# Hybrid attention trunk with 64 experts: the rank of a token is mapped to a partition in steps of seven

## Chip, core and metric

One Trainium2 chip, one core. The metric is device time in microseconds (us), the median of the runs shown. Nothing else runs on the chip.

## What is computed

A batch of one sequence: 2048 tokens of width 1024, behind 16 learned meta tokens. One layer:

1. `u = rmsnorm(h)`, `z = u @ w_in`; `z` is split for two groups of heads. Four heads are gated linear attention over chunks of 64 (`gla_group`), four are latent attention with softmax (`mla_group`). Both outputs go through `w_out` and are added to `h`.
2. `rmsnorm(h)` is routed in two steps: the best of 8 groups, then the best 2 of the 8 experts of that group, with gates from the two softmaxes. Each of the 64 experts is a SwiGLU of width 512, and its output times the gate is added to `h`:

```
hdn = silu(xb @ w_gate[e]) * (xb @ w_up[e])
out[token] += gate * (hdn @ w_down[e])
```

3. A last `rmsnorm`, without the meta tokens.

All is float32. Every token has two experts, so there are 4096 pairs of token and expert. Routing the given inputs by the reference gives between 23 and 109 tokens for an expert, 64 on average. No expert has more than the 112 that a block of the kernel holds.

## The kernel before

The program runs in phases. `phase_z` makes `z`, `phase_g` the linear attention, `phase_mix` the latent attention, the output projection and the routing. `phase_moe` runs the 64 experts, in the order group 0's first expert, group 1's first, and so on. Float32 products are made of two halves each, `hi` (the value rounded to a shorter type) and `lo` (the rest), three matmuls for one.

**Routing.** For each pair of token and expert the kernel counts how many earlier tokens chose that expert: the rank. A row of numbers `iob` (128 partitions by `BS` = 112 columns, the same in every partition) is written once, on GpSimd, at line 761. At line 1035 each rank is compared with `iob`: `R` has a one in the column whose number is the rank. Matmuls with `R` on the left (lines 1046, 1110 and 1113) then carry token number, gate, norm factor and a flag (is this expert the token's first) to the partition that has the number of that column. The results are `rt["src"]` and `tab`: for each expert a column of 112 partitions. A partition with no token keeps the number 2048, which lies past the last row.

```
1035:  R[:, k] = (rank[:, k, js, None] == iob)      # in short
1680:  B = [block(xsb[i % XSB], ..., rt["src"][:, e:e + 1], e, i) ...]
```

**Rows of tokens.** Each expert has four indirect DMAs, issued by GpSimd, all with one token row (4 KB) to a partition and 112 partitions: `gather(S.xs, S.src, ud)` reads the normed rows, `gather(S.b, S.src, hz)` reads the sums so far, `spread(hz, zd, S.z)` writes the new sums for the tokens whose first expert this is, `spread(out, od, S.o)` writes the finished rows for the others. A row number past 2047 moves no row (`bounds_check`). So an expert with n tokens moves n rows in `xs`, n in `b`, and n in `hz` and `out` together. The rank decides which of the 112 partitions have a row.

**Weights.** An expert has six tiles `raw` of 1 MB (128 partitions by 8 KB): gate, up and down, two each. SyncE loads them (line 1320) into a ring of six (`RAWB`); a load is issued once its buffer has been read. ScalarE makes `hi` of a tile, VectorE makes `lo` (line 1335 and the `Ordered` wrapper, whose instructions all have line 124), TensorE multiplies. The second `down` tile is used as float32, without halves. Per expert that is 60 matmuls of 512 columns in halves (48 `pg`, 12 `pd`), 8 float32 passes (`pd<-raw,hc`), and 12 transposes (8 `pt`, 4 `pth`).

**Order.** `moe_plan` writes one list of the instructions of all engines for the 64 experts; each engine runs its own in that order. On VectorE the small instructions that TensorE needs (`xl`, the low half of the turned token rows, and `hl`) stand between the large `lo`.

The loop `For_i(0, again, 1)` behind the experts serves experts of more than 112 tokens; here it runs no pass. It uses `iob` too (line 1766).

Of the kernel before, what the change touches and what calls it, by code (L numbers as in the profile page):

```python
# [34 lines left out]
BS = 112  # L35
# [40 lines left out]
def build(tc, a, dbg=None, stop=99):  # L76
    nc = tc.nc
    dbg = dbg or {}
    with ExitStack() as top:
# [23 lines left out]
        with ExitStack() as ctx:  # L103
            env["ctx"] = ctx
            env["keep"] = ctx.enter_context(tc.tile_pool(name="keep", bufs=1))
            z_rest, z_close = phase_z(**env)
            env["right"] = right = ExitStack()
            kvp = right.enter_context(tc.tile_pool(name="kv", bufs=1, side=RIGHT))
            env["kv"] = ([kvp.tile([P, L], F32R, name=n) for n in ("ch", "cl", "kr_")]
                         + [kvp.tile([P, NT + 1, P], F32R, name=n) for n in ("vh", "vl")])  # L110
            g_rest, g_close = phase_g(z_rest=z_rest, z_close=z_close, **env)
            phase_mix(g_rest=g_rest, g_close=g_close, **env)
            phase_moe(**env)
# [644 lines left out]
def phase_mix(tc, nc, a, qd, qrd, hg, ud, hz, xlist, xexp, kv, ident, ones, eps, rt, keep, ctx, right, g_rest, g_close, **_):  # L758
    ch, cl, kr_, vh, vl = kv
    iob = keep.tile([P, 1, BS], F32, name="iob")  # L760
    nc.gpsimd.iota(iob, pattern=[[0, 1], [1, BS]], base=0, channel_multiplier=0, allow_small_or_imprecise_dtypes=True)
    ids = keep.tile([P, 2, NT], F32, name="ids")
    nc.gpsimd.iota(ids, pattern=[[SEQ, 2], [P, NT]], base=-FAR, channel_multiplier=1, allow_small_or_imprecise_dtypes=True)
    rank = keep.tile([P, 2, NT], F32, name="rank")
# [1115 lines left out]
```

## Time and profile before

| | us |
|---|---|
| median of 3 runs (lowest, highest) | 2520.22 (2518.09, 2521.58) |
| profiled execution | 2517.44 |
| its span, first to last instruction | 2515.7 |
| mean granted TensorE clock | 0.98 |

The profile comes from one execution. A row of a group gives its busy time and what ended the idle time before it. Matmuls overlap, so the duration of one is longer than the distance from one to the next; how fast TensorE really goes is read from the starts in the timeline. The experts take the second half of the span: `silu` of the first starts at 1222.8 us, that of the 64th at 2479.9 us.

### The profile page before, as it was taken

The numbers are of one execution on the slowest core, as the hardware profiler recorded it, in microseconds if no ns is written. First come the engines' busy times: TensorE is split into PE (matmuls) and PEld (weight loads), VectorE is DVE, ScalarE is ACT, GpSimd is POOL, SyncE is SP. The second block draws the span as 40 slices with busy tenths as digits, with TensorE's granted clock in tenths as the row PEclk, the third lists the DMA queues.
The fourth block names the chain that finished last, engine by engine and source line by source line (L and its number), as shares of the span: only waits on it lengthen the run. The fifth ranks groups of instructions, "written<-read, shape, count | busy, mean of one in ns | idle before, by whom it ended". The sixth has DMA issues, their size and how long they took to land. (4 is left out here: it accounts for less than half of the span.)

```text
span 2515.7 us, 35600 instructions
## 1 busy us (share of the span) xinstructions
PE 2371.7 (94%) x12897; PEld 1876.6 (75%) x12897; DVE 1761.5 (70%) x2756; ACT 1307.3 (52%) x2018; POOL 816.6 (32%) x740
## 2 busy tenths in 40 slices
PE   7999998899999999998799999999999999999997
PEld 7899997687789999898566666666666666676664
DVE  6334244777577777776677778887877788787785
ACT  5112103554365555555466666666665666666663
POOL 0000003621001111112355545454445544454443
PEclk9999999899999999999799999999999999999999
DMA  6212116554412122113899999999999999999994
GB/s 208 74 59 80 54 44 174 174 173 143 165 55 77 60 68 71 65 51 141 251 368 361 349 352 353 358 353 361 355 342 350 344 351 360 354 348 363 344 358 182
DMA packets 161154, 571.70 MB, mean 227 GB/s; under 512 B 37132, under 2 KB 79644, under 8 KB 111820
## 3 DMA queue, kind: packets, MB, share of 16 engines
q1 hardware_dynamic: 125612, 509.71, 56.9%
q0 software_dynamic: 32912, 50.94, 6.3%
q10 hardware_dynamic: 2448, 8.72, 1.1%
q8 instruction: 103, 1.69, 0.3%
q14 instruction: 79, 0.65, 0.1%
HBM read 529.71 MB, written 106.63 MB: 253 GB/s over the span
## 5 line engine op out<-in xcount | busy, mean ns | idle before, releaser
L124 ACT CAST hi<-raw 128x2048 fp32r<-128x2048 f32 x318 | 607.0, 1909 | 444.0 <-DMA raw<-in_w_gate_dram 216.8
L124 DVE TENSOR_TENSOR lo<-raw,hi 128x2048 fp32r<-128x2048 f32 x317 | 723.5, 2287 | 136.4 <-ACT hi L124 131.1
L124 PE MATMUL pg<-hi,xl 128*112 128x512 f32 x1024 | 415.6, 406 | 50.1 <-DVE xl L124 50.1
L124 PE MATMUL pg<-hi,xh 128*112 128x512 f32 x1024 | 435.5, 425 | 2.0 <-ACT xh L124 1.8
L124 PE MATMUL pg<-lo,xh 128*112 128x512 f32 x1024 | 406.6, 397 | 0.0
L124 POOL DMA_INDIRECT hz<-z,t_zd x64 | 195.1, 3049 | 463.1 <-DVE z L124 454.4
L124 PEld LDWEIGHTS pg<-hi,xl 128*112 128x112 f32 x1024 | 181.6, 177 | 125.0 <-DVE xl L124 67.2
L124 PEld LDWEIGHTS pg<-hi,xh 128*112 128x112 f32 x1024 | 182.1, 178 | 73.5 <-ACT xh L124 15.1
L124 PEld LDWEIGHTS pg<-lo,xh 128*112 128x112 f32 x1024 | 182.8, 179 | 68.0 <-issue 7.8
L124 PE MATMUL pd<-raw,hc 128*112 128x512 f32 x512 | 230.0, 592 | 0.0
L135 PE MATMUL ps<-uh,wh 128*128 128x256 f32 (+3 forms) x768 | 219.1, 286 | 0.7 <-ACT uh L223 0.7
L136 PE MATMUL ps<-ul,wh 128*128 128x256 f32 (+3 forms) x768 | 218.8, 285 | 0.0
L137 PE MATMUL ps<-uh,wl 128*128 128x256 f32 (+3 forms) x768 | 218.0, 284 | 0.0
L124 PEld LDWEIGHTS pd<-raw,hc 128*112 128x112 f32 x512 | 90.0, 176 | 104.2 <-issue 97.0
L124 DVE SCALAR_TENSOR_TENSOR o<-z,ss,gain 112x1024 f32<-112x1024 f32 x64 | 82.2, 1285 | 118.5 <-POOL ss L124 118.5
L124 POOL DMA_INDIRECT out_dram<-o,t_od x64 | 121.3, 1895 | 105.0 <-DVE hl L124 88.8
L124 POOL DMA_INDIRECT xs<-ud,src x64 | 136.3, 2130 | 44.6 <-PE pt L124 22.3
L135 PEld LDWEIGHTS ps<-uh,wh 128*128 128x128 f32 (+1 forms) x768 | 145.2, 189 | 1.5 <-ACT uh L223 1.1
L136 PEld LDWEIGHTS ps<-ul,wh 128*128 128x128 f32 (+1 forms) x768 | 145.2, 189 | 0.6 <-DVE ul L224 0.2
L137 PEld LDWEIGHTS ps<-uh,wl 128*128 128x128 f32 (+1 forms) x768 | 145.3, 189 | 0.1
L257 DVE COPY st<-ps 128x256 f32<-128x256 f32 (+1 forms) x64 | 27.0, 422 | 145.7 <-PE ps L137 145.7
L338 POOL TENSOR_SCALAR_AFFINE_SELECT mf<-ones 128x128 f32<-128x128 f32 x2 | 0.6, 302 | 380.2 <-PE ps L137 380.2
(2413 smaller groups left out, 5340.8 us busy)
## 6 DMA issues: line engine op xcount, KB each, us to landing
raw<-in_w_gate_dram SPq DMA_DIRECT2D x128, 1024.0 KB
raw<-in_w_up_dram SPq DMA_DIRECT2D x128, 1024.0 KB
raw<-in_w_down_dram SPq DMA_DIRECT2D x128, 1024.0 KB
x<-in_x_dram SPq DMA_DIRECT2D x32, 512.0 KB
zf<-st SPq DMA_DIRECT2D x85, 128.0 KB
hg<-x SPq DMA_DIRECT2D x16, 512.0 KB
x<-hg SPq DMA_DIRECT2D x16, 512.0 KB
hz<-x SPq DMA_DIRECT2D x16, 512.0 KB
```

What stands on the lines that cost most here:

```text
L124: return self.tc.keep_in_program_order(f(*args, **kw))
L135: nc.tensor.matmul(out, lh, rh, start=start, stop=False, **kw)
L136: nc.tensor.matmul(out, lh, rl, start=False, stop=False, **kw)
L137: nc.tensor.matmul(out, ll, rh, start=False, stop=stop, **kw)
L257: nc.vector.tensor_copy(st[:w, :n - o], ps[:w, :n - o])
L338: nc.gpsimd.affine_select(mf[:, :, hh], ob, pattern=[[CH, 2], [1, CH]], compare_op=OP.is_ge, fill=0.0, base=0, channel_multiplier=-1)
```

## The change

The row `iob` gets other numbers. Before, column c held c. Now the 112 columns are seen as 16 groups of 7, and column 7e + r holds e + 16 r (e from 0 to 15, r from 0 to 6). A token of rank 0 goes to partition 0, rank 1 to partition 7, rank 2 to 14, rank 15 to 105, rank 16 to partition 1, and so on. Each of the 112 numbers still occurs once.

```
-    nc.gpsimd.iota(iob, pattern=[[0, 1], [1, BS]], base=0, channel_multiplier=0, allow_small_or_imprecise_dtypes=True)
+    nc.gpsimd.iota(iob.rearrange("p o (e r) -> p (o e) r", e=16), pattern=[[1, 16], [16, BS // 16]], base=0, channel_multiplier=0, allow_small_or_imprecise_dtypes=True)
```

No other line changes, and on every engine the instructions stand in the same order as before, with the same shapes. What differs is which of the 112 partitions hold a token's row in each expert's block, and so which partitions of the four indirect DMAs move 4 KB.

## Rows read from the trace of the kernel before

**Rows 1.** Busy time by stretch: weights, the experts' start, their steady part.
```profile
core 0: us, PE busy (x) PEld busy (x) DVE busy (x) ACT busy (x) POOL busy (x), PEclk, DMA share, GB/s
1180.00:1200.00 20.00, 10.59 (x73) 9.14 (x71) 17.53 (x46) 12.02 (x19) 4.12 (x8) 0.75 1.00 405
1260.00:1300.00 40.00, 38.50 (x164) 26.48 (x163) 32.13 (x24) 25.11 (x24) 21.12 (x11) 1.00 1.01 374
1300.00:2400.00 1100.00, 1047.41 (x4382) 721.22 (x4382) 879.29 (x659) 683.51 (x656) 547.49 (x331) 0.99 0.98 353
```

**Rows 2.** The tile sg, one silu per expert: duration, first and last start.
```profile
L124 ACT ACTIVATE sg<-pg,tab x64: 672/682/697, 1222.8 to 2479.9; 112x512 f32<-112x512 f32 x64
```

**Rows 3.** TensorE and VectorE in order of time: start, duration, idle before, releaser.
```profile
1703.01 1.04 PE L124 MATMUL pt<-ident,xs 112*128 112x112 f32 x8
...
1706.64 3.59 PE L124 MATMUL pd<-raw,hc 128*112 128x512 f32 x8
...
1712.72 0.49 PE L124 MATMUL pg<-hi,xl 128*112 128x512 f32 x1 [2.02 <-DVE xl L124]
1713.05 0.39 PE L124 MATMUL pg<-hi,xh 128*112 128x512 f32 x1
...
1717.68 0.39 PE L124 MATMUL pg<-hi,xl 128*112 128x512 f32 x1
1717.92 0.55 PE L124 MATMUL pth<-ident,h 112*128 112x112 f32 x4
1718.23 0.46 PE L124 MATMUL pg<-hi,xh 128*112 128x512 f32 x1
```

**Rows 4.** ScalarE and VectorE just before, in the same form.
```profile
1706.96 1.90 ACT L124 CAST hi<-raw 128x2048 fp32r<-128x2048 f32 x1 [1.63 <-DMA raw<-in_w_gate_dram]
...
1708.89 2.29 DVE L124 TENSOR_TENSOR lo<-raw,hi 128x2048 fp32r<-128x2048 f32 x1 [1.43 <-ACT hi L124]
...
1711.10 1.12 DVE L124 SCALAR_TENSOR_TENSOR h<-pg,grs,sg 112x512 f32<-112x512 f32 x1
...
1712.06 0.61 DVE L124 TENSOR_TENSOR xl<-pt,xh 128x448 fp32r<-128x448 f32 x1
```

**Rows 5.** Waits from 1300 to 2400 us: total, times, longest.
```profile
ACT hi L124 <- DMA raw<-in_w_gate_dram: 198.7, 89, 4.3
DVE lo L124 <- ACT hi L124: 116.9, 113, 2.4
ACT hi L124 <- DMA raw<-in_w_up_dram: 106.0, 93, 2.2
ACT hi L124 <- DMA raw<-in_w_down_dram: 73.8, 46, 3.1
PE pg L124 <- DVE xl L124: 44.3, 32, 2.1
```

**Rows 6.** DMA queues, 1183 to 1199 us: packets, MB, share of 16 engines.
```profile
DMA packets 1062, 6.65 MB, mean 416 GB/s; under 512 B 122, under 2 KB 122, under 8 KB 378
q1 hardware_dynamic: 1062, 6.65, 101.3%
```

**Rows 7.** The same from 1300 to 2400 us.
```profile
DMA packets 75573, 388.22 MB, mean 353 GB/s; under 512 B 23033, under 2 KB 23033, under 8 KB 33423
q1 hardware_dynamic: 47351, 344.81, 85.7%
q0 software_dynamic: 28160, 42.63, 11.9%
```

**Rows 8.** Four stretches of 10 us at the end, columns as in rows 1.
```profile
2440.00:2450.00 10.00, 9.70 (x49) 7.32 (x48) 6.80 (x5) 5.69 (x7) 7.93 (x5) 1.00 0.96 395
2450.00:2460.00 10.00, 10.00 (x38) 6.29 (x37) 9.97 (x9) 8.35 (x8) 1.63 (x1) 1.00 0.92 310
2460.00:2470.00 10.00, 9.79 (x49) 7.43 (x48) 6.78 (x6) 4.96 (x7) 7.55 (x5) 1.00 0.99 405
2470.00:2480.00 10.00, 10.00 (x41) 6.41 (x40) 10.00 (x9) 8.15 (x10) 2.90 (x2) 1.00 0.93 326
```

**Rows 9.** The instruction that is changed.
```profile
L761 POOL IOTA iob<- x1: 233/233/233, 1.1 to 1.1; 128x112 f32 x1
```

## The prediction, made before the result was known

> **What bounds the kernel now.** I read the busy times by stretch first, then the waits, then one stretch in order of time, then the DMA queues. The change can only act where the partition of a token matters, in the experts. Their 63 steps from the first silu to the last take 2479.9 - 1222.8 = 1257.1 us, 19.95 us each [rows 2]. That is half of the span, and the only part that I let move.
>
> TensorE is busy for 1047.41 of 1100 us there [rows 1], so it looks like the bound. Matmul durations overlap, so I counted starts. From 1713.05 to 1717.68 there are 20 steps in 4.63 us, 0.2315 us a matmul [rows 3]. An expert has 60 of them, 13.9 us; the 8 float32 passes take about 3.4 us (3.59 less the overlap of the last), the 8 transposes pt 1.04, and the 4 of pth 0.31 (17.92 to 18.23). With 0.1 for a slow first matmul this is 18.8 us. So about 1.15 us of each step is time in which TensorE issues nothing. The profile shows 1100 - 1047.41 = 52.6 us idle in some 55 experts, 0.96 us each, of which xl alone ended 44.3 us [rows 1, 5].
>
> Why is xl late? The reader should follow one case backwards. TensorE stood 2.02 us until xl, which ran at 1712.06 [rows 3, 4]. VectorE runs in its written order, and before xl stood a lo that could start only at 1708.89, since it waited for hi, which started at 1706.96 when a gate tile had landed; ScalarE had been idle for 1.63 us [rows 4]. So a late weight tile delays lo, lo delays xl, xl delays TensorE. ScalarE waited for weights 198.7 + 106.0 + 73.8 = 378.5 us in this stretch [rows 5], a third of it. The weight loads set the pace, with TensorE 6% behind.
>
> **The DMA's rate.** From 1300 to 2400 us 388.22 MB moved at 353 GB/s [rows 7]: some 7.08 MB a step, 6.29 of weights and 192 rows of 4 KB (64 tokens, three rows each). Just before the experts, with weights and two plain stores but no indirect row under way, the same engines moved 416 GB/s [rows 6]. At that rate a step's bytes would need 17.0 us, and weights would never be late. With the token rows the rate swings: 395, 310, 405, 326 in four stretches of 10 us [rows 8]. The share of busy DMA time is 0.98 [rows 1], which looks like 16 full engines. It need not be: an engine that has a packet of each queue open counts both. A weight packet of 8 KB took 358 ns here (85.7% of 16 x 1100 us, over 344.81 MB / 8 KB) against 319 ns before the experts (101.3% of 16 x 16 us, over 6.65 MB) [rows 6, 7]. So this share can't tell whether the row traffic slows all engines or only fills some.
>
> **The change, part by part.** The iota writes the same 112 numbers in another order; it took 0.233 us at the start of the program [rows 9], and a nested pattern costs at most some tenths there, beside the first loads. Nothing else is added, removed or moved on any engine; no wait is added. R, tab and all matmuls have the same shapes, with zeros in other places.
>
> What changes is which partitions of the four indirect DMAs carry 4 KB. I assume that an indirect DMA of 112 partitions gives each of the 16 engines seven neighbours. No view says so; it is the step on which the forecast stands. [...]
>
> Before: ranks 0 to n-1 fill the partitions from 0 up. Any expert with at least 7 tokens fills the first engine: 7 rows of xs, 7 of b, and 7 of hz and out together, 21 rows of 4 KB a step. With 64 tokens the first nine engines carry nearly all rows and the last six none. After: engine e holds the ranks with rest e modulo 16, so 64 tokens put 4 + 4 + 4 = 12 on each engine; over the 64 experts' own counts the fullest engine averages 13.6.
>
> Price of a packet from rows 6: 416 / 16 = 26 GB/s for an engine, 315 ns for 8 KB, 158 for 4 KB. A load of 1 MB is 128 packets, 8 for an engine, 48 a step.
> - Fullest engine before: 48 x 0.315 + 21 x 0.158 = 15.12 + 3.32 = 18.44 us. Measured step: 19.95, so 1.5 us (8%) are empty packets, gaps and slow packets.
> - Emptiest before: 15.1 us. It can run ahead by at most the loads that the six buffers allow, and then stands. A tile has landed only when its slowest engine is through.
> - After: 15.12 + 12 x 0.158 = 17.0 (17.3 for the fullest). With the same extra, added or in proportion, 18.4 to 18.8 us.
>
> So the weight path falls from 19.95 to about 18.6, just under TensorE's 18.8, which becomes what is late next. Both being nearly equal, and experts having 23 to 109 tokens, I do not expect TensorE without gaps: I add 0.3 us (a third of its present 0.96 idle) and take 19.1 us a step. That needs 7.08 / 19.1 = 371 GB/s; the best 40 us with rows under way held 374 [rows 1].
>
> Sum: 63 x (19.95 - 19.1) = 53.6 us from the profiled execution's 2517.4 gives 2463.8. That execution was 2.8 us under the median of the runs, so 2466.
>
> Bounds of the step: not under TensorE's 18.8 (63 x 1.15 = 72 us, 2448), perhaps 0.1 less where its clock no longer dips (0.99 in the stretch), 2441. From above, if half of the gain is eaten by packets that remain slow, 19.5 (28 us), 2492.
>
> **The rivals.**
> 1. *Row traffic slows all engines alike, or the memory is the ceiling.* For it: 0.98 busy, 353 GB/s flat for 1100 us, and longer packets [rows 1, 7]. Against it: 405 and 416 without indirect rows, and 374 for 40 us with them [rows 1, 6]. Then spreading the rows changes only how long they are under way: the step stays at 19.7 to 19.95, 2504 to 2520. [...]
> 2. *The change doesn't do what it says:* engines take partitions in turn (p modulo 16). Then the rows were spread before (64 partitions, 4 to an engine, 12 rows a step) and are after: 2520. Against it: by the prices above every engine would then need 17.0 us, and TensorE, not the weights, would have been late, unless rival 1 holds as well.
> 3. *Slower.* Now every engine carries both queues, and none is free to run ahead with weights. Place: the landing of the raw tiles. If the alternation of 4 KB and 8 KB packets costs rate, and not the number of packets, the 310 to 326 GB/s of the stretches with most row traffic [rows 8] would hold for all engines and longer. It decides once the mean falls under today's 353: at 340, 20.8 us a step, 0.87 more, +55 us, 2575. Against it: the rows are under way for a shorter time when each engine has 4 of them and not 7, and their number is the same.
>
> **How the numbers follow.** Forecast (steps of 18.7 to 19.5, 2441 to 2492) 0.80. Rival 1: 0.12, of which 0.08 still gains more than 0.2% (5 us, about what a measurement of this kernel can tell from no change) and 0.04 does not. Rival 2: 0.04, no change. Rival 3: 0.04, slower. So faster 0.88, same 0.08, slower 0.04. The range leaves out the last of the forecast's lower end and the unchanged cases: 2441 to 2505.
>
> **What would show it.** Silu to silu near 19.1 us. ScalarE's waits for raw far below 378 us per 1100, xl's wait on TensorE below half of 44.3. DMA at 365 to 375 GB/s, with the 10 us swings smaller. A weight packet's mean time may stay or grow, since more engines then have both queues open; that alone says nothing. Xs and b should land sooner after their issue. The first 1180 us should not move. Wrong if the rate stays at 353 with the same waits (rivals 1 and 2) or falls (rival 3); a rate above 360 with TensorE as idle as before would mean that xl waits for something other than weights.

## The result and the profile after

| us | before | after |
|---|---|---|
| median (lowest, highest) | 2520.9 (2518.09, 2522.79), 4 runs | 2450.09 (2446.82, 2460.98), 4 runs |
| ratio, 95% interval | | 0.9733 [0.9718, 0.9749] |
| profiled execution, its span | 2517.44, 2515.7 | 2446.82, 2445.1 |

The changed kernel is 2.7% faster. First the time of a step, in the tile sg of the changed kernel (duration in ns, first and last start), which answers to [rows 2]:
```profile
L124 ACT ACTIVATE sg<-pg,tab x64: 680/690/707, 1222.7 to 2410.4; 112x512 f32<-112x512 f32 x64
```
The first silu starts where it did, 1222.7 against 1222.8 us. The 63 steps behind it take 1187.7 us and not 1257.1: 18.85 us each and not 19.95. Those 69.4 us are all but one of the 70.6 us that the span lost.

Busy time by stretch, the same stretches and columns as [rows 1]:
```profile
1180.00:1200.00 20.00, 10.12 (x73) 8.68 (x72) 18.15 (x46) 11.90 (x19) 4.12 (x8) 0.85 1.01 403
1260.00:1300.00 40.00, 40.00 (x174) 28.35 (x173) 34.13 (x27) 26.91 (x27) 23.08 (x15) 1.00 1.02 392
1300.00:2400.00 1100.00, 1092.34 (x4661) 761.08 (x4660) 926.70 (x697) 722.93 (x697) 669.32 (x347) 1.00 1.00 375
```
TensorE is idle for 7.7 of 1100 us, before for 52.6 [rows 1]. Its granted clock is 1.00 there, before 0.99. The rate rose from 353 to 375 GB/s, although the share of busy DMA time hardly moved (0.98 to 1.00): that share did not show what was wrong before. By the times of the packets in the trace more than 16 of them are open at once in 20% of the 1100 us before and in 23% after, so with 16 engines the share counts some engine time twice.

The longest waits of ScalarE, and the one of TensorE, from 1300 to 2400 us (total, times, longest), answering to [rows 5]:
```profile
ACT hc L124 <- DVE hl L124: 191.8, 58, 5.0
ACT hi L124 <- PE pg L124: 112.9, 54, 3.7
ACT hi L124 <- DMA raw<-in_w_gate_dram: 42.7, 42, 2.9
ACT hi L124 <- DMA raw<-in_w_up_dram: 11.1, 21, 1.2
PE pd L124 <- DVE hl L124: 7.7, 38, 0.3
ACT hi L124 <- DMA raw<-in_w_down_dram: 6.1, 4, 2.3
```
ScalarE waits for weights 59.9 us, before 378.5. It now waits more for TensorE to give a buffer back, and most for hl, the low half of the hidden rows. So the order of cause has turned: weights held TensorE up before, TensorE holds the weights up now. Xl no longer ends any wait of the matmul queue PE; hl does, in 38 experts.

What TensorE needs by itself is seen in the first part of the stretch:
```profile
1300.00:1640.00 340.00, 340.00 (x1467) 240.17 (x1466) 293.74 (x219) 229.64 (x220) 202.24 (x110) 1.00 1.02 383
1640.00:2400.00 760.00, 752.34 (x3195) 520.91 (x3194) 632.97 (x479) 493.29 (x478) 467.08 (x238) 1.00 0.99 372
```
Up to 1640 us it is never idle, and from the first pt of an expert to that of the next it takes 18.57 to 18.59 us (18 steps, by the starts in the trace). The 40 steps behind them take 19.04 on average, the more coming from one wait for hl in 38 of them. One of those late cases, on GpSimd, VectorE and TensorE:
```profile
1702.74 4.98 POOL L124 DMA_INDIRECT hz<-z,t_zd  x1 [4.77 <-DVE z L124]
1708.02 0.99 POOL L124 DMA_INDIRECT b<-hz,src  x1 [0.30 <-issue]
...
1710.01 1.29 DVE L124 SCALAR_TENSOR_TENSOR o<-z,ss,gain 112x1024 f32<-112x1024 f32 x1 [3.15 <-POOL ss L124]
1711.21 0.38 DVE L124 TENSOR_TENSOR hl<-pth,hh 128x224 fp32r<-128x224 f32 x1
...
1709.97 1.04 PE L124 MATMUL pt<-ident,xs 112*128 112x112 f32 x8
1710.78 0.46 PE L124 MATMUL pd<-hi,hh 128*112 128x512 f32 x1
1711.08 0.40 PE L124 MATMUL pd<-lo,hh 128*112 128x512 f32 x1
1711.65 0.49 PE L124 MATMUL pd<-hi,hl 128*112 128x512 f32 x1 [0.18 <-DVE hl L124]
```
GpSimd finishes ss (the factor of the last rmsnorm) behind its two indirect DMA instructions; VectorE waits for ss before o, and hl stands behind o in its order; TensorE waits for hl. From 1711.08 to the next matmul it takes 0.57 us and not the usual 0.23, of which the profile counts 0.18 as idle, since the matmul before runs on for 0.40. In the 18 short steps hz takes 2.8 us and hl is there in time.

The DMA queues in the same stretch, answering to [rows 7], and four stretches of 10 us at the end of the experts, to [rows 8]:
```profile
DMA packets 80043, 412.49 MB, mean 375 GB/s; under 512 B 24324, under 2 KB 24324, under 8 KB 35155
q1 hardware_dynamic: 50434, 367.20, 87.1%
q0 software_dynamic: 29542, 44.44, 12.5%
```
```profile
2370.00:2380.00 10.00, 9.75 (x49) 7.39 (x48) 6.80 (x5) 4.84 (x7) 7.82 (x5) 1.00 1.00 410
2380.00:2390.00 10.00, 10.00 (x39) 6.34 (x38) 9.97 (x9) 8.40 (x8) 2.12 (x1) 1.00 0.88 302
2390.00:2400.00 10.00, 9.75 (x49) 7.40 (x48) 6.82 (x5) 4.82 (x6) 7.07 (x5) 1.00 1.01 410
2400.00:2410.00 10.00, 10.00 (x41) 6.40 (x40) 9.97 (x9) 8.30 (x9) 2.90 (x2) 1.00 0.89 312
```
A weight packet takes 87.1% of 16 x 1100 us over 367.20 MB / 8 KB = 342 ns, before 358. The swing within a step is as large as it was; why is told further down. And the changed instruction, to [rows 9]:
```profile
L761 POOL IOTA iob<- x1: 472/472/472, 1.1 to 1.1; 128x112 f32 x1
```
The nested pattern costs 0.24 us more, at 1.1 us after the start, and nobody waits for it.

**A second reading of the trace: how far apart the shares of one load land.** The trace keeps 16 semaphore increments for most loads of a weight tile, at different times. I read each as the share of one of the 16 engines; no view names the engine that an increment comes from. The load counts as landed with the last of them: of the 274 hi that start from 1300 to 2400 us before, 211 do so 77 to 110 ns behind the 16th increment of a load. From first to last of them, averaged over the loads of 1300 to 2400 us that have all 16 (296 of 328 before, 319 of 343 after), I worked out 7.98 us before and 2.37 after. With a load every 3.3 us (a sixth of 19.95), the first shares were more than two loads ahead of the last. The table of the experiments has this number in a column. The prediction did not argue from it.

### The profile page after: what moved, and what is told of

The parts are those of the page before. It is cut to its first block, busy times and chain, and to the rows that moved or that the text cites. A ratio compares the mean times of both kernels' runs of the same rounds, so it can differ in the third digit from the quotient of the medians.

```text
span 2445.1 us, 35600 instructions
## 1 busy us (share of the span) xinstructions
PE 2350.4 (96%) x12897; PEld 1870.6 (77%) x12897; DVE 1755.0 (72%) x2756; ACT 1303.9 (53%) x2018; POOL 905.4 (37%) x740
## 5 line engine op out<-in xcount | busy, mean ns | idle before, releaser
L124 PE MATMUL pg<-hi,xl 128*112 128x512 f32 x1024 | 407.6, 398 | 2.7 <-DVE xl L124 2.7
L124 POOL DMA_INDIRECT hz<-z,t_zd x64 | 262.0, 4094 | 323.2 <-DVE z L124 314.5
L124 POOL DMA_INDIRECT out_dram<-o,t_od x64 | 193.6, 3025 | 105.0 <-DVE hl L124 82.4
L124 POOL DMA_INDIRECT xs<-ud,src x64 | 126.6, 1978 | 40.7 <-issue 18.7
```

Of the source, the lines that this page charges most:

```text
L124: return self.tc.keep_in_program_order(f(*args, **kw))
```

## The experiments

Theory S, on which the prediction stood: each of the 16 engines serves a block of seven neighbouring partitions of an indirect DMA, and the engine with the most rows sets the pace of the weights. "Rows" is the count of 4 KB rows a step on the fullest engine by that theory, from the routing of the given inputs. "Fours" is the same count by another grouping, that of rivals F and N: two blocks of four neighbouring partitions, 32 apart in the same half of 64, are one group. It is a way of counting that the runs below put to the test, no more. Both are averaged over the 64 experts for each engine or group, and then the fullest is taken. (Where another one is the fullest from expert to expert, the fullest of each has more: by fours 16.5 and not 16.0 after, 17.1 and not 12.6 in e8.)

No view shows which engine moves which row, but the increments of one early gather speak for theory S. It is the second xs, for an expert with 57 tokens, issued near 1210 us, before the first silu. Its 16 increments come in an early and a late group, and the early one is as large as the number of engines that theory S leaves without a row or with a single one:

| order of ranks | shares that land early | without a row by blocks of seven | by blocks of eight | by fours |
|---|---|---|---|---|
| plain (before) | 8, by 3.1 us; the others from 4.0 us on | 7, and one with a single row | 8, and one with a single row | 8 |
| e4_deal10 | 6, by 2.4 us; the others from 3.5 us on | 6 | 7 | 7 |
| e3_deal12 | 4, by 2.2 us; the others from 3.3 us on | 4 | 5, and one with a single row | 3, and one with a single row |
| e2_step8 | no group, all from 3.0 us on | 0 | 2 | 7 |
| after | no group, all from 3.1 us on | 0 | 2 | 1 |

Blocks of eight neighbours, which the steps below alone do not exclude, fall by it. All runs:

| run | rows | fours | step, us | first to last share, us | us waited for weights | GB/s |
|---|---|---|---|---|---|---|
| before | 21.0 | 23.8 | 19.95 | 7.98 | 378 | 353 |
| e1_reverse | 21.0 | 23.8 | 19.84 | 8.01 | 369 | 355 |
| e4_deal10 | 18.8 | 21.3 | 19.50 | 7.23 | 338 | 362 |
| e3_deal12 | 17.0 | 19.3 | 19.17 | 5.92 | 269 | 369 |
| e2_step8 | 15.0 | 23.2 | 19.30 | 5.94 | 301 | 365 |
| e9_fours | 13.6 | 23.3 | 19.19 | 5.40 | 299 | 369 |
| after | 13.6 | 16.0 | 18.85 | 2.37 | 60 | 375 |
| e12_after | 13.6 | 16.0 | 19.01 | 2.00 | 36 | 372 |
| e10_ring7 | 21.0 | 23.8 | 19.85 | 11.08 | 352 | 355 |
| two matmuls of three: | | | | | | |
| e5_two_before | 21.0 | 23.8 | 20.09 | 8.35 | 362 | 350 |
| e8_two_sevens | 21.0 | 12.6 | 20.29 | 8.58 | 373 | 347 |
| e7_two_fours | 13.6 | 23.3 | 19.22 | 6.27 | 311 | 367 |
| e6_two_after | 13.6 | 16.0 | 19.00 | 2.62 | 81 | 372 |

The step is the distance from the first to the last start of sg over 63; the rate is that of 1300 to 2400 us. Waited for weights is the sum of the three waits of hi for raw there. Each row of the table is one profile; two profiles of the same changed kernel differ by 0.16 us in the step (after and e12_after), so smaller differences between two rows say little by themselves.

**e1_reverse: the ranks from the other end.**
```
-nc.gpsimd.iota(iob, pattern=[[0, 1], [1, BS]], base=0, ...)
+nc.gpsimd.iota(iob, pattern=[[0, 1], [-1, BS]], base=BS - 1, ...)
```


> Column c of iob holds 111 - c: rank 0 goes to partition 111, rank 1 to 110, and so on. Theory S (each of 16 engines takes seven neighbouring partitions of an indirect DMA, and the engine with the most rows sets the pace of the weights): the fullest engine still has 21 rows a step, only it is the last and not the first. Step 19.95 us, time 2520 within 6 us. Rival P (the low partitions, or the engines that serve them, were the trouble, since other things go there too): the rows move away from them, 2450 to 2500. Rival O (any other order of the rows in memory helps): faster than 2510.

Measured: 2513.8 us, ratio 0.9979 [0.9963, 0.9994]; tile sg:
```profile
L124 ACT ACTIVATE sg<-pg,tab x64: 672/681/697, 1227.5 to 2477.6; 112x512 f32<-112x512 f32 x64
```
A step of 1250.1 / 63 = 19.84 us. The crowd of rows at the high partitions costs the same as at the low ones. Neither the place nor another order as such is what the change gains by: rivals P and O fall.

**e2_step8: ranks eight partitions apart.**
```
+nc.gpsimd.iota(iob.rearrange("p o (e r) -> p (o e) r", e=14), pattern=[[1, 14], [14, BS // 14]], base=0, ...)
```


> Column 8e + r holds e + 14 r: rank 0 to partition 0, rank 1 to 8, rank 2 to 16, rank 14 to 1. The rows that fall to the fullest engine, counted from the routing and averaged over the 64 experts, are: by theory S (blocks of seven neighbours) 15.0 a step, against 21.0 before and 13.6 after the change. By rival F (blocks of four partitions, 64 apart on the two halves) 23.2, against 23.8 before. By rival M (partition modulo 16) 21.0, against 13.6 before. So theory S: step 18.9 to 19.0 us, 2455 to 2463 us. Rival F: 2510 to 2521. Rival M: not faster than before, by its own count 7.4 rows of 0.158 us more a step, up to 2590.

Measured: 2484.3 us, ratio 0.9874 [0.9849, 0.9899]:
```profile
L124 ACT ACTIVATE sg<-pg,tab x64: 676/686/707, 1226.6 to 2442.8; 112x512 f32<-112x512 f32 x64
```
19.30 us a step. This is between the theories. Faster than before, so the engines do not take partitions modulo 16 (rival M), and blocks of four alone (rival F) do not decide. But it is 21 us slower than theory S had at most. The count of rows on an engine is not all.

**e3_deal12 and e4_deal10: the ranks dealt over 12 or 10 blocks of seven.**
```
+for n, c0, c1 in ((12, 0, 84), (4, 84, BS)):       # e4: ((10, 0, 70), (6, 70, BS))
+    nc.gpsimd.iota(iob[:, :, c0:c1].rearrange("p o (e r) -> p (o e) r", e=n), pattern=[[1, n], [n, 7]], base=c0, ...)
```


> The ranks are dealt as in the change, but over the first 12 blocks of seven partitions; the other four blocks are filled after those 84. The fullest engine has 17.0 rows a step by theory S. 15.12 us for weight packets + 17.0 x 0.158, and the 8% or 1.5 us that the step before had on top: 19.27 to 19.32 us, 2478 to 2482 us, between before and after. Rival E (what costs is that some engines run dry, whichever rows the fullest has): four engines are still nearly without rows, so no gain or hardly any, 2505 to 2521.

> As the kernel that deals over 12 blocks, with 10. Theory S: 18.8 rows on the fullest engine, step 19.57 to 19.60 us, 2496 to 2500 us: with the runs of 12, 16 and the plain order a line of some 63 x 0.158 x 1.08 = 10.7 us for each row until TensorE's 18.85 us binds. Rival E: 2515 to 2521.

Measured: 2469.8 us, ratio 0.9816 [0.9792, 0.9841], and 2491.0 us, ratio 0.9905 [0.9876, 0.9934]. Tile sg of 12, then of 10:
```profile
L124 ACT ACTIVATE sg<-pg,tab x64: 674/686/702, 1222.8 to 2430.2; 112x512 f32<-112x512 f32 x64
```
```profile
L124 ACT ACTIVATE sg<-pg,tab x64: 672/683/699, 1224.5 to 2453.0; 112x512 f32<-112x512 f32 x64
```
19.17 and 19.50 us, against 19.27 to 19.32 and 19.57 to 19.60 expected. The gain comes in proportion, also while by theory S four or six engines still have hardly any rows: rival E falls. From 21.0 to 17.0 rows the step falls by 0.79 us, 0.20 us a row, some more than the 0.17 that the forecast's price of a row, 0.158 us, and its 8% gave. In these runs the fours fall along with the rows, so they can't be told apart here.

**e5 to e8: TensorE's work cut by a third, two orders that part the two counts.** In the experts the matmul of the low half of the token rows (or of the hidden rows) with the high half of the weights is left out:
```
+def mm2(on, out, lh, ll, rh, rl, start, stop):
+    on.tensor.matmul(out, lh, rh, start=start, stop=False)
+    on.tensor.matmul(out, lh, rl, start=False, stop=stop)
```
e5 has the plain order of ranks and e6 the changed one. e7 deals to the blocks of seven as the change does, but takes the partitions with `(p >> 2) & 1 == 0` of each block first. e8 fills whole blocks of seven in the order that the expectation names.

> The plain order of ranks, and in the experts two of the three matmuls of a product: the one with the low half of the token rows (or of the hidden rows) is left out. TensorE's step falls by 20 x 0.2315 us to some 14.2, so that what the weights alone allow can be read. If the weights set the pace before, the step stays at 19.8 to 20.0 us from silu to silu, and the time at 2505 to 2521 us. If TensorE's own work had a part in it, the step falls, to 19 or less.

> The same cut with the changed order of ranks. After the change TensorE bounds the step at 18.85 us; without it the weights should show their own pace. By theory S (only the rows of the fullest engine count: 13.6) 18.7 us. By theory C (rows of the fullest engine, and rows that land in the four-partition blocks that the same engine's weights are written to; fitted on the five steps 19.95, 19.84, 19.50, 19.30 and 19.17 as 16.09 + 0.102 x the largest sum of own rows + 0.7 x block rows) 18.6 us. Rival V (VectorE's 15.9 us of work in its written order binds next): no lower than 18.85 with VectorE over 90% busy.

> Two of three matmuls, as above. Each block of seven still gets the ranks e, e + 16, ..., so the engines' rows are those of the change (13.6 on the fullest). But inside a block the partitions with an even number of fours come first (0 to 3, 8 to 11, 16 to 19, ...), so that counted by blocks of four, 64 apart, the fullest has 23.3 rows, as the plain order (23.8; the change 16.0). Theory S: 18.7 us a step, as the changed order. Theory C: 19.1 us. Rival N (the blocks of four alone decide): 19.9.

> Two of three matmuls. The opposite: the ranks fill whole blocks of seven as in the plain order (21.0 rows on the fullest engine), but the blocks are taken in the order 12, 11, 3, 13, 4, 2, 5, 10, 14, 6, 1, 9, 0, 15, 7, 8, by which every block of four gets 10.8 to 12.6 rows. Theory S: 19.95 us a step. Theory C: 19.1 us. Rival N: 18.5 us.

Measured, median and ratio to before: e5 2534.3, 1.0087 [1.0056, 1.0117]; e6 2458.2, 0.9777 [0.975, 0.9805]; e7 2475.1, 0.9834 [0.9804, 0.9863]; e8 2540.4, 1.0092 [1.0056, 1.0128]. Tile sg of e5, e6, e7 and e8:
```profile
L124 ACT ACTIVATE sg<-pg,tab x64: 679/682/693, 1230.4 to 2496.0; 112x512 f32<-112x512 f32 x64
```
```profile
L124 ACT ACTIVATE sg<-pg,tab x64: 680/692/694, 1226.2 to 2423.3; 112x512 f32<-112x512 f32 x64
```
```profile
L124 ACT ACTIVATE sg<-pg,tab x64: 680/691/693, 1222.7 to 2433.5; 112x512 f32<-112x512 f32 x64
```
```profile
L124 ACT ACTIVATE sg<-pg,tab x64: 676/682/695, 1228.8 to 2506.9; 112x512 f32<-112x512 f32 x64
```
e5 settles what bounded the kernel before: with 20 matmuls a step less the step is not shorter (20.09 us), so TensorE's own work did not set it. e8 against e5 settles what the rows must be spread over: with the fours evened out and the sevens crowded the step stays at 20.29. Theory C, which I had fitted to five steps, expected 19.1 and falls; so does rival N. (The blocks to which theory C has an engine write its weights are an assumption of that theory; no run shows them.) Theory S holds there. e7 against e6 says that the fours do count once the sevens are even: 0.22 us.

e6 did not do what it was for. I wanted the weights' own pace, but other waits took over, as the waits of e6 from 1300 to 2400 us show:
```profile
ACT hc L124 <- DVE hl L124: 261.8, 57, 5.9
...
PE pd L124 <- ACT hc L124: 150.2, 58, 2.7
...
ACT hi L124 <- DMA raw<-in_w_gate_dram: 56.4, 37, 2.8
```
TensorE waits for hc, ScalarE for hl, and hl stands in VectorE's written order; the granted clock is 0.93 in that stretch with TensorE busy for 906 of 1100 us. VectorE is busy for 83%, so rival V's 90% did not come either. What the weights alone would need with the rows spread stays open; it is not over 18.6 us, the pace that they kept up with in the first 18 steps of the changed kernel.

**e9_fours: the order of e7 with all three matmuls.**
```
+for e in range(16):
+    own = sorted(range(7 * e, 7 * e + 7), key=lambda p: ((p >> 2) & 1, p))
+    ...   # column own[j] gets the rank e + 16 j
```


> All three matmuls, each block of seven dealt as in the change (13.6 rows on the fullest engine), but inside a block the partitions with an even number of fours first, so that by blocks of four the fullest has 23.3 rows (the change 16.0). With two matmuls this order took 19.22 us a step, the change's 19.00, where the weights were not the only thing waited for. If crowding into blocks of four costs by itself, the step is 19.2 us, above TensorE's 18.85, and the time some 20 us over the changed kernel's of this call. If only the rows of an engine count: 18.85, and no difference from the changed kernel beyond 5 us.

Measured: 2470.1 us, ratio 0.9812 [0.9796, 0.9829], against 0.975 [0.9734, 0.9766] for the changed kernel on the same chip:
```profile
L124 ACT ACTIVATE sg<-pg,tab x64: 676/686/699, 1225.1 to 2434.1; 112x512 f32<-112x512 f32 x64
```
19.19 us, as expected, and 14 us over the changed kernel there (20 expected). Its waits for weights from 1300 to 2400 us are back:
```profile
ACT hi L124 <- DMA raw<-in_w_gate_dram: 176.7, 74, 4.8
ACT hi L124 <- DMA raw<-in_w_up_dram: 65.5, 69, 2.2
ACT hi L124 <- DMA raw<-in_w_down_dram: 56.4, 38, 3.1
```
So the partitions inside a block of seven matter too. What it is about them no view shows.

**e10_ring7: a ring of seven weight tiles, plain order.**
```
-RAWB = 6
+RAWB = 7
```


> The plain order of ranks with a ring of seven weight tiles and not six. Theory S: the fullest engine always has loads queued, so one more buffer only lets the others run further ahead: step 19.9 to 20.0 us, time within 6 us of before. Rival B (tiles are late because a load can't be issued until a buffer is free): one more load in flight hides up to 3 us a tile, and TensorE's 18.85 us shows, 2450 to 2480.

Measured: 2512.9 us, ratio 0.9987 [0.9975, 0.9999]:
```profile
L124 ACT ACTIVATE sg<-pg,tab x64: 671/682/702, 1228.2 to 2478.7; 112x512 f32<-112x512 f32 x64
```
19.85 us a step. The first shares of a load land 11.08 us ahead of the last and not 7.98, one load more, and that is all the seventh buffer does. The step is no shorter for it: before has 19.95 and e1 19.84.

**e11_half: no float32 down tile.**
```
-NATIVE = ("d1",)
+NATIVE = ()
```


> The changed order, and the second down tile in halves like the other five: 12 matmuls of 0.2315 us, 2.78, in place of 8 passes of 0.43, 3.44. TensorE's step falls by 0.66 us to 18.2. ScalarE gets one more hi (1.91 us), VectorE one more lo (2.29 us): VectorE 15.9 + 2.3 - 0.4 (the hidden rows' low half grows) is about 18.2 us a step, the weights some 18.6. If TensorE is what binds the changed kernel, this can gain up to 0.3 us a step, 20 us, and if VectorE without slack is worse than TensorE without slack it is slower by 0 to 60 us. I take slower: 18.9 to 19.5 us a step.

Measured: 2765.7 us, ratio 1.0982 [1.0964, 1.1]:
```profile
L124 ACT ACTIVATE sg<-pg,tab x64: 675/682/696, 1229.3 to 2735.7; 112x512 f32<-112x512 f32 x64
```
23.91 us a step, far over the 18.9 to 19.5 that I took. No wait for weights is left among the long ones (first lines of its waits, 1300 to 2400 us):
```profile
ACT hi L124 <- PE pd L124: 362.1, 93, 7.9
...
PE pd L124 <- DVE hl L124: 171.0, 46, 5.3
```
Six tiles a step go through four buffers of hi, and hi waits for matmuls that wait for hl. That is a chain of its own, so the run says nothing on how much a shorter step of TensorE would be worth.

**e12_after: the changed kernel on the chip of those three.**

> The changed kernel once more, beside the three others on the same chip: step 18.85 us, ratio to before 0.973 within 0.003.

Measured: 2456.2 us, ratio 0.975 [0.9734, 0.9766], step 19.01 us:
```profile
L124 ACT ACTIVATE sg<-pg,tab x64: 678/688/700, 1227.2 to 2424.7; 112x512 f32<-112x512 f32 x64
```
The ratio is as expected, the step 0.16 us longer. Here hz takes 5.0 us in every step of 1300 to 2400 us, and TensorE waits for hl in 57 of 58:
```profile
PE pd L124 <- DVE hl L124: 11.7, 57, 0.3
```
The weights aren't the reason: ScalarE waits 36 us for them, less than in the other profile. No order tried beats the changed kernel.

## Why the prediction was right

2450 against 2466 forecast, inside the range, and by the steps that were named; in two of its terms errors went unpunished.

- *The weights bound the experts before.* Shown: e5 has a quarter less of TensorE's work and no shorter step.
- *Blocks of seven, and 21 rows on the fullest.* This was assumed. No run shows which engines a DMA of 112 partitions uses, nor seven neighbours to each, from which the sum has its 21, 12 and 13.6 rows; in its place the runs showed 16 increments for most gathers and steps that go with these counts. e1, e4, e3, and e8 against e5 bear it out: where the fullest block of seven has 21 rows the step is 19.8 to 20.3 us, whatever the place or order, and it falls with the rows; the shares of the early gather fit no other assignment that was counted. It is not the whole: e2 and e9, with 15.0 and 13.6 rows but crowded fours, take 19.30 and 19.19. The sum had no term for that. It went unpunished by luck: the step of seven that the change takes also lowers the fours, from 23.8 to 16.0.
- *The weight path at 18.4 to 18.8 us after.* Not measured by itself (e6 was to do it); from 1300 to 1640 us the weights kept up with 18.6.
- *TensorE next, at 18.8 us.* TensorE is next, with the waits of hi for raw nearly gone, but it needs 18.57 to 18.59 us. The sum counted the eight pt with their duration, 1.04 us [rows 3], where the next matmul starts after 0.81 (1709.97 to 1710.78 above). That is 0.23 us too much, of the kind that the sum had set out to avoid by counting starts.
- *0.3 us a step of remaining gaps.* The size came out, 18.85 - 18.58 = 0.27, the reason did not, so this is luck: the term stood for late weights, and what TensorE waits for is hl, behind GpSimd's ss. The forecast was 16 us too slow, 63 x (19.1 - 18.85) = 15.8, and the 0.23 us of pt is nearly all of that.
- *Rate of 365 to 375 GB/s:* 375. *Xl's wait below half of 44.3 us:* gone on PE.
- *Smaller 10 us swings:* wrong. 410, 302, 410, 312 after, where [rows 8] had 395, 310, 405, 326. It isn't what rows under way allow, as rival 1 would have it. Two stretches of 2 us inside the one with 302, and SyncE's waits from 2360 to 2400:
```profile
2380.00:2382.00 2.00, 2.00 (x10) 1.37 (x9) 1.97 (x2) 2.00 (x3) 2.00 (x1) 1.00 0.48 152
2386.00:2388.00 2.00, 2.00 (x10) 1.52 (x9) 2.00 (x2) 0.41 (x2) 0.00 (x0) 1.00 1.03 410
SPq L1320 <- DVE lo L124: 28.7, 9, 6.6
```
From 2386 to 2388 us the core moved 410 GB/s, with 0.32 of its 0.82 MB in the queue of the indirect DMAs. Around 2380 the weights ran dry: SyncE issued no load from 2374.3 to 2380.9, since no buffer was free.
- *Rival 1, a ceiling:* against it the mean of 375 GB/s over 1100 us, where it was 353 before.
- *Rival 2, partitions in turn:* against it e2, which by that count would have had 21.0 rows for 13.6 and was faster. *Rival 3, slower:* its mean below 353 did not come.
- *Xs and b landing sooner:* right. From the issue to the last of the 16 increments, where all are kept, xs takes 8.5 us on average after and 11.3 before, b 9.7 and 10.7.

## What to carry to other kernels

In this kernel the filled rows of padded gathers and scatters stood together, and the last share of a weight load came 8.0 us behind the first; with the rows dealt out it came 2.4 us behind, and the step fell from 19.95 to 18.85 us. That the crowded rows put their bytes on some DMA engines only, and that the loads then landed at the pace of the fullest, is theory S, which these runs bear out in the main and no view shows. Where a kernel has such gathers, try dealing the filled rows over all partitions; it costs one constant. A mean busy share of 0.98 hid the trouble here. What showed it is the distance between the first and the last share of one large load, and a consumer that waited for loads (378 us of 1100) although their mean rate, 353 GB/s, was below the 416 seen elsewhere in the trace. Look for the price where the loads bound a stage: once another engine binds (here TensorE, never idle at 18.6 us a step), more evenness has little left to give. And look then at what the binding engine waits for: here the next 0.27 us a step, by estimate 63 x 0.27 = 17 us, lie in a chain that begins on GpSimd, an engine that is busy for 669 of 1100 us. No run here took that chain away.

## What was not expected of the hardware

- Which partitions inside a block of seven carry rows matters: 0.2 to 0.3 us a step (e7 against e6, e9 against after and e12), with the same number of rows in every block.
- GpSimd's indirect DMA instruction to hz takes 1.0, 2.8 or 5.0 us and seldom anything between, and in the changed kernel it is what TensorE ends up waiting for. It takes about 5.0 us in 15 of 64 experts before, in 40 after and in 60 in e12_after. The order of the rows alone does not set it, since the changed kernel has both, first the short and then the long form. In its trace the wait for hl begins one step after hz has changed from 2.8 to 5.0 us and stays. That the one causes the other is read from the trace; no run changes hz by itself, and what makes it change is open.

Means before and after, from the page's groups:
```profile
L124 POOL DMA_INDIRECT hz<-z,t_zd x64 | 195.1, 3049 | 463.1 <-DVE z L124 454.4
```
```profile
L124 POOL DMA_INDIRECT hz<-z,t_zd x64 | 262.0, 4094 | 323.2 <-DVE z L124 314.5
```
